# Where a decoder's modulation products stand between its memory attention and its feed-forward

## The chip, the cores and the metric

One core of a Trainium2 chip runs one program. The metric is the device time of one execution in microseconds, as a median of runs. Lower is better.

## The reference, cut to what matters

A first block (sequence of 512 tokens, width 1024) does a mixer, a cross-attention to a memory, and a feed-forward, each added to x. Two layers of a second block follow. Each layer is steered by three vectors (shift, scale, gate) for the tokens and three for a context; they come from a small product of a conditioning vector with `w_mod`, and depend on nothing else.

```python
x = x + memory_cross_attention(rms_norm(x, norm_mem_g), mem, ..., w_mo)   # ends with o @ w_mo
h = rms_norm(x, norm_ffn_g)
x = x + square(relu(h @ w_ff1)) @ w_ff2
...
sc, scc = silu(c), silu(c_ctx)
for i in range(2):
    mod_x = sc @ w_mod[i] + b_mod[i]        # 1024 x 3072
    mod_c = scc @ w_mod[i] + b_mod[i]
    x, ctx = mixer_layer(x, ctx, mod_x, mod_c, ...)
```

## The kernel before, in words

**Weights.** All weights are fp32 in HBM and pass through one stream (class `Stream`, lines 184 to 330). A chunk of 512 KB is loaded into a raw slot by SyncE's queue (L205, `loads`); there are 3 slots at first, 7 from the memory's attention on and 9 after the memory's output projection (`more_raw`). A chunk is split into a high and a low part: one unit of 512 columns (fp32r weights, L266 on ScalarE and L267 on VectorE), or one unit of 1024 columns (feed-forward, fp16, L273 on ScalarE and two L291 on VectorE). The units live in a ring of 9 (`RING`), so a unit can be made only when the one nine before it has been used up by TensorE. A raw slot is free again when its units are split. A product takes three matmuls: high by high, low by high, high by low (L416, L417, L418).

**Scales.** An fp16 unit can be made only when its group of columns has a scale: the sum of squares of each of the group's four chunks is taken on ScalarE (L224, written into the ring tile of the unit just being made, so in two halves of 512 where that unit is fp32r), then `total` adds them up (L428 on VectorE, L430 a small matmul, L431, L432 on GpSimd, L433) and L273 may begin. `pump` takes these sums while it makes units, and looks ahead by four chunks at most:

```python
while n and self.nstat < self.nd and self.nstat <= ci + AHEAD:   # L258, AHEAD = 4
    n -= self.stat(lo)
```

**Order.** The program is a list of steps. A clock kept by hand (`D.clk`) advances by each matmul's estimated cost; at each tick `pump` may make one unit, and chains that are due take their next step (`norm_chain` waits `N1` = 2000 and `ND` = 1300 of it). The frame that builds the program then orders each engine's instructions by its own model of time, so neighbours on an engine can change places.

**The modulation pieces.** `w_mod` of a layer is taken in 6 pieces of 1024 by 512, twelve in all (`mod`, L1439). A piece is four chunks, eight fp32r units (8 of L266, 8 of L267), 16 matmuls of 512 columns (L1444, L1445, L1447), one eviction (L1451, L1452) and one small write on ScalarE's queue (L1453). Nothing reads a layer's six results before all six are there; then `mod_chain` (L1458) works them up and writes `mod_d`. `MODS` names for each of the twelve the place in the program where it stands:

```python
MODS = 'duuhhhhii012'                     # L49
mods = [(n, (1, n) if n < 6 else (0, n - 6)) for n in range(12)]
```

Four stand in the memory's attention (`h`). Two stand between the memory's output projection and the feed-forward (`i`, L2372). One each stands at the ends of the feed-forward's parts 0, 1 and 2.

**Around the change.** The memory's output projection takes two blocks of 512 columns over four token tiles; a token tile of a block is 12 matmuls. With the second block, each tile's sum is added to x (L1238) and its norm begins at once (`norm_x`, `norm_chain`): a square with its sum on ScalarE (L614), six short instructions on GpSimd (L404 to L412), one multiplication on VectorE (L618), eight transposes on TensorE (L630), two copies on ScalarE (L421) and two subtractions on VectorE (L422). Two buffers hold the normed tile, so tile 2 begins when tile 0 has been transposed. Then come the pieces of `i`, then part 0 of the feed-forward's first matrix (`ff1`, L1364), whose first block works on tokens 0 to 255 first (tiles 0 and 1, 48 matmuls of 256 columns), then on tokens 256 to 511. The feed-forward has eight parts of 512 hidden columns, in the order ff1(0), ff1(1), ff2(0), slot 0, ff1(2), ff2(1), slot 1, and so on; after part 4 the context's norm is set up (`ctx_norm0`, L1497), which needs layer 0's six pieces.

Of the kernel before, what the change touches and what calls it, by code (L numbers as in the profile page):

```python
# [45 lines left out]
ZP = 2  # L46
ZPOS = ((0, 0), (0, 1), (0, 2), (4, 0), (4, 2), (4, 3), (5, 3), (5, 4), (6, 2), (7, 3))
VPOS = ((1, 1), (1, 2), (1, 3), (2, 1), (2, 2), (2, 3))
MODS = 'duuhhhhii012'  # L49
RN = 1.2  # L50
RM = 2.24
RA = 0.6
# [279 lines left out]
def decoder_kernel(ctx: ExitStack, tc: tile.TileContext, A: dict, out: bass.AP):  # L332
# [1973 lines left out]
    def add_mod(i, j):  # L2306
        add(lambda b: mod(i, j, b), wblk(A["w_mod_2"][i][:, j * 512:(j + 1) * 512], fr=True))
# [3 lines left out]
    def slot(c):  # L2311
        while mods and MODS[mods[0][0]] == c:
            add_mod(*mods.pop(0)[1])
# [131 lines left out]
```

## Time and profile before

| what | value |
|---|---|
| median of 3 runs | 2428.55 us (2423.89 to 2429.85) |
| the profiled execution | 2421.47 us |
| its span, first to last instruction | 2419.7 us |
| mean granted TensorE clock | 0.978 of full speed |
| VectorE, ScalarE, GpSimd busy | 64%, 54%, 13% of the span |
| DMA | 226.67 MB, 94 GB/s over the span |

The span is the time that the trace covers; the execution's own time has 1.77 us around it. Times in rows are microseconds from the span's start. In the timeline, the length of a matmul includes its run through the array, and the next one starts before it ends: the pace is the distance of starts. A number in square brackets is the time for which the engine sat idle before the row, with the instruction that ended it.

### The profile page before, as it was taken

What the parts mean: (1) busy time and instruction counts of PE and PEld (TensorE: products, weight loads), DVE (VectorE), ACT (ScalarE), POOL (GpSimd) and SP (SyncE); (2) the same over time, 40 slices, a digit from 0 to 9 for tenths busy, and PEclk for the clock granted to TensorE, in tenths of its full rate; (3) what the DMA queues carried; (4) which work ended last, traced back from release to release, by engine and by line L of the source; (5) the groups of instructions that cost most, each with busy time, mean ns of one, the idle gap of its engine ahead of it and who ended that gap; (6) DMA issues with size and microseconds to landing.
All of it is one profiled execution on the core that took longest, in us unless ns stands there. A gap on an engine that the chain in (4) does not pass through costs nothing. (4 is left out here: it accounts for less than half of the span.)

```text
span 2419.7 us, 38066 instructions
## 1 busy us (share of the span) xinstructions
PE 2261.3 (93%) x14342; PEld 1505.2 (62%) x14342; DVE 1544.2 (64%) x3136; ACT 1298.1 (54%) x2745; POOL 320.7 (13%) x703
## 2 busy tenths in 40 slices
PE   7899899899999989999988999999779999899998
PEld 6777687544444557767767566557546567764446
DVE  6878678656665677665777444443777657865543
ACT  5656457746655455535777434323535457775532
POOL 4320321100100211004000000000621121000001
PEclk9899899899999999999999999999989999999999
DMA  4512445534443411112221422211421113233311
GB/s 158 140 47 71 141 144 199 172 101 153 155 140 106 122 50 38 46 40 65 79 74 56 137 79 61 79 42 63 156 86 50 42 38 108 71 115 113 103 44 61
DMA packets 182220, 226.67 MB, mean 94 GB/s; under 512 B 28556, under 2 KB 130876, under 8 KB 182036
## 3 DMA queue, kind: packets, MB, share of 16 engines
q1 hardware_dynamic: 158084, 187.67, 25.1%
q10 hardware_dynamic: 23952, 36.57, 4.4%
q8 instruction: 112, 1.84, 0.3%
q14 instruction: 72, 0.59, 0.1%
HBM read 207.33 MB, written 16.88 MB: 93 GB/s over the span
## 5 line engine op out<-in xcount | busy, mean ns | idle before, releaser
L416 PE MATMUL mm<-hTh,wh 128*128 128x512 f16 (+1 forms) x1040 | 392.6, 378 | 7.3 <-ACT wh L273 3.1
L291 DVE SCALAR_TENSOR_TENSOR wl<-raw,gs,wh 128x512 f16<-128x512 f32 (+2 forms) x420 | 296.6, 751 | 150.6 <-ACT wl L224 116.5
L417 PE MATMUL mm<-hTl,wh 128*128 128x512 f16 (+1 forms) x1040 | 392.4, 377 | 0.0
L418 PE MATMUL mm<-hTh,wl 128*128 128x512 f16 (+1 forms) x1040 | 391.2, 377 | 0.0
L224 ACT ACTIVATE wl<-raw 128x1024 f16<-128x1024 f32 (+3 forms) x242 | 222.9, 921 | 69.6 <-PE mm L417 37.3
L416 PEld LDWEIGHTS <-wh 128*128 128x128 f16 x1712 | 168.0, 98 | 147.4 <-issue 6.8
L417 PEld LDWEIGHTS <-wh 128*128 128x128 f16 x1712 | 168.0, 98 | 146.1 <-issue 9.6
L418 PEld LDWEIGHTS <-wl 128*128 128x128 f16 x1712 | 167.8, 98 | 143.9 <-issue 0.6
L738 ACT ACTIVATE ph<-mm 128x512 f16<-128x512 f32 (+2 forms) x300 | 146.1, 502 | 162.4 <-PE mm L734 156.1
L273 ACT ACTIVATE wh<-raw,gs 128x1024 f16<-128x1024 f32 x156 | 175.3, 1141 | 105.9 <-PE mm L417 83.0
L266 ACT ACTIVATE wh<-raw 128x512 fp32r<-128x512 f32 (+2 forms) x244 | 141.7, 613 | 142.2 <-PE mm L418 49.7
L739 DVE SCALAR_TENSOR_TENSOR pl<-mm,ph 128x512 f16<-128x512 f32 (+2 forms) x300 | 165.9, 567 | 73.6 <-ACT ph L738 71.1
L267 DVE TENSOR_TENSOR wl<-raw,wh 128x512 fp32r<-128x512 f32 (+2 forms) x244 | 156.1, 667 | 55.3 <-ACT wh L266 40.2
L432 POOL TENSOR_TENSOR gs<-gs,nh 128x1 f32<-128x1 f32 x66 | 40.6, 616 | 1125.2 <-DVE gs L431 1079.3
L416 PE MATMUL mm<-wh,hTh 128*128 128x512 f32 (+5 forms) x512 | 181.7, 356 | 5.5 <-DVE vf L1589 2.0
L418 PE MATMUL mm<-wh,hTl 128*128 128x512 f32 (+5 forms) x512 | 180.1, 352 | 1.8 <-DVE hTl L422 1.7
L417 PE MATMUL mm<-wl,hTh 128*128 128x512 f32 (+5 forms) x512 | 180.1, 352 | 0.3 <-DVE wl L267 0.3
L734 PE MATMUL mm<-ident,P 128*128 128x128 f32 x928 | 153.9, 283 | 5.9 <-ACT P L721 2.0
L721 ACT ACTIVATE P<-S,s 128x768 f32<-128x768 f32 (+4 forms) x160 | 105.8, 666 | 35.1 <-PE mm L734 18.0
L734 PEld LDWEIGHTS mm<-ident,P 128*128 128x128 f32 x928 | 108.6, 145 | 19.6 <-ACT P L721 2.9
L2133 DVE SCALAR_TENSOR_TENSOR z<-z,mm 128x256 f32<-128x256 f32 (+1 forms) x72 | 42.8, 596 | 107.2 <-PE mm L418 98.9
L271 POOL TENSOR_SCALAR wh<-raw,gs 128x1024 f16<-128x1024 f32 (+3 forms) x54 | 65.8, 1219 | 328.2 <-PE mm L417 209.9
(503 smaller groups left out, 5360.8 us busy)
## 6 DMA issues: line engine op xcount, KB each, us to landing
raw<-in_w_in_dram SPq DMA_DIRECT2D x124, 512.0 KB, 3.5
raw<-in_w_ff_dram SPq DMA_DIRECT2D x64, 512.0 KB, 4.5
raw<-in_w_mod_dram SPq DMA_DIRECT2D x48, 512.0 KB, 5.1
raw<-in_w_branch_dram SPq DMA_DIRECT2D x24, 512.0 KB, 3.4
raw<-in_w_o_dram SPq DMA_DIRECT2D x16, 512.0 KB, 4.0
raw<-in_cmp_w_dram SPq DMA_DIRECT2D x16, 256.0 KB, 3.5
raw<-in_w_out_dram SPq DMA_DIRECT2D x8, 512.0 KB, 3.6
raw<-in_w_mkv_dram SPq DMA_DIRECT2D x8, 512.0 KB, 3.7
```

Of the source, the lines that this page charges most:

```text
L224: nc.scalar.activation(lo[:, :b - a], t[:, a:b], AF.Square, accum_out=g.t[:, g.cols:g.cols + 1])
L266: nc.scalar.activation(hi[:, :m], src, AF.Copy)
L267: nc.vector.tensor_sub(lo[:, :m], src, hi[:, :m].bitcast(FT))
L273: nc.scalar.activation(hi[:, :m], src, AF.Copy, scale=s)
L291: self.nc.vector.scalar_tensor_tensor(l[:, b], src[:, b], s, h[:, b], op0=OP.mult, op1=OP.subtract)
L416: PE.matmul(ps, ah, bh, start=start, stop=False)
L417: PE.matmul(ps, ah, bl, start=False, stop=False)
L418: PE.matmul(ps, al, bh, start=False, stop=stop)
L721: ACT.activation(P, v[:, j, :], AF.Exp, bias=it.nb[:, j:j + 1], accum_out=it.den[:, j:j + 1])
L734: PE.transpose(ps[:, a - a0, :], it.P[0 if len(it.P) == 1 else j][:, c:c + 128], ident)
L738: ACT.activation(ph[:, :m], ps[:, :m], AF.Copy, scale=PSC)
L739: DVE.scalar_tensor_tensor(pl[:, :m], ps[:, :m], PSC, ph[:, :m], op0=OP.mult, op1=OP.subtract)
```

## The change

Only the string of places differs.

```diff
-MODS = 'duuhhhhii012'
+MODS = 'duuhhhh00123'
```

The pieces keep their order. Layer 0's pieces 1 and 2, which stood at `i`, go to the end of part 0; piece 3 goes from the end of part 0 to that of part 1, piece 4 from part 1 to part 2, and piece 5 from part 2 to part 3. Seen by places, `i` has none instead of two, part 0 ends with two instead of one, parts 1 and 2 end with one as before, and part 3 ends with one instead of none. The stream loads weights in the order of use, so the eight chunks of the two pieces are loaded behind the twelve of ff1(0), ff1(1) and ff2(0) instead of ahead of them, and the sums of squares for ff1(0) are taken while the units of the memory's output projection are made.

## Rows read from the trace of the kernel before

**Rows 1.** The page, part 1: busy us (share of the span) xinstructions.
```profile
PE 2261.3 (93%) x14342; PEld 1505.2 (62%) x14342; DVE 1544.2 (64%) x3136; ACT 1298.1 (54%) x2745; POOL 320.7 (13%) x703
```

**Rows 2.** By stretch: us; PE, PEld, DVE, ACT, POOL busy; clock, DMA share, GB/s.
```profile
443.06:468.87 25.81, 14.96 (x67) 8.46 (x66) 18.52 (x36) 23.31 (x51) 4.30 (x14) 0.77 0.51 164
468.87:482.00 13.13, 13.13 (x97) 10.74 (x97) 11.53 (x21) 12.24 (x19) 0.00 (x0) 0.79 0.69 236
482.00:533.66 51.66, 51.66 (x244) 23.45 (x242) 24.68 (x48) 21.68 (x42) 1.10 (x2) 1.00 0.28 93
533.66:537.55 3.89, 3.89 (x18) 1.53 (x16) 2.55 (x4) 3.72 (x5) 0.00 (x0) 1.00 0.46 135
```

**Rows 3.** Timeline, TensorE: start us, us, line, out<-in xcount [idle before <-releaser].
```profile
444.69 1.03 PE L630 MATMUL S<-ident,xn 128*128 128x128 f32 x8
...
449.43 0.39 PE L1444 MATMUL mm<-wh,ms 128*34 128x512 f32 x1
453.59 1.72 PE L630 MATMUL S<-ident,xn 128*128 128x128 f32 x8 [3.77 <-DVE hTl L422]
...
460.49 0.63 PE L1444 MATMUL mm<-wh,ms 128*34 128x512 f32 x1
...
468.87 0.39 PE L416 MATMUL mm<-hTh,wh 128*128 128x256 f16 x1 [3.06 <-ACT wh L273]
...
474.57 0.27 PE L416 MATMUL mm<-hTh,wh 128*128 128x256 f16 x1
```

**Rows 4.** Timeline: norm of tile 0, of tile 3; splits by source.
```profile
435.86 1.06 ACT L614 ACTIVATE xn<-oc 128x1024 f32<-128x1024 f32 x1 [3.04 <-DVE oc L1238]
...
438.89 0.19 POOL L412 TENSOR_TENSOR s<-s,s 128x1 f32<-128x1 f32 x1
...
439.12 1.28 DVE L618 SCALAR_TENSOR_TENSOR xn<-oc,s,g 128x1024 f32<-128x1024 f32 x1 [0.68 <-POOL s L412]
...
453.06 1.04 ACT L614 ACTIVATE xn<-oc 128x1024 f32<-128x1024 f32 x1
...
L421 ACT ACTIVATE hTh<-S x8: 575/580/597, 447.2 to 463.7; 128x512 f16<-128x512 f32 x8
```

**Rows 5.** Timeline, ScalarE: sums of squares (L224), splits (L266), scaling (L273).
```profile
443.86 0.61 ACT L224 ACTIVATE wl<-raw 128x512 fp32r<-128x512 f32 x1
...
444.47 1.67 ACT L266 ACTIVATE wh<-raw 128x512 fp32r<-128x512 f32 x3
...
458.63 0.62 ACT L224 ACTIVATE wl<-raw 128x512 fp32r<-128x512 f32 x1
...
467.68 8.41 ACT L273 ACTIVATE wh<-raw,gs 128x1024 f16<-128x1024 f32 x8
```

**Rows 6.** Timeline, ScalarE and TensorE around the end of part 0.
```profile
532.75 0.63 ACT L266 ACTIVATE wh<-raw 128x512 fp32r<-128x512 f32 x1 [7.45 <-PE mm L418]
533.83 1.06 ACT L224 ACTIVATE wl<-raw 128x1024 f16<-128x1024 f32 x1 [0.45 <-PE mm L417]
...
546.63 0.17 PE L430 MATMUL S<-sb,onesb 128*128 128x1 bf16 x1
...
547.80 4.27 ACT L273 ACTIVATE wh<-raw,gs 128x1024 f16<-128x1024 f32 x4 [1.00 <-POOL gs L432]
```

**Rows 7.** Timeline, VectorE and TensorE, where the context's norm is put.
```profile
660.78 1.28 DVE L618 SCALAR_TENSOR_TENSOR xn<-ctx,s,g 128x1024 f32<-128x1024 f32 x1 [4.00 <-DMA g<-mod_d]
...
663.12 0.38 PE L416 MATMUL mm<-wh,ffh 128*128 128x512 f16 x1 [2.93 <-DVE oc L1240]
```

**Rows 8.** Weight loads: one issue on SyncE's queue, and issue to landing.
```profile
413.24 9.60 SPq L205 DMA_DIRECT2D raw<-in_w_mod_dram  x7
...
DMA to landing us min/median/max: 3.6/5.2/5.5
```

**Rows 9.** Timeline, TensorE in the memory's attention: a gap, and matmuls after it.
```profile
388.15 0.38 PE L416 MATMUL S<-mkh,mqh 128*128 128x256 f32 x1 [2.01 <-ACT P L721]
...
390.76 0.41 PE L418 MATMUL S<-mkh,mql 128*128 128x256 f32 x1
```

## The prediction

> **What bounds the kernel now.** The first view is the page's busy times: TensorE works through 93% of the span [rows 1], so a change that adds and removes no work can only win or lose where TensorE waits or runs at half clock. The second is the table by stretch. From ff1(0)'s second half to the end of ff2(0) TensorE never stops and has its full clock: 51.66 us for 240 matmuls of 512 columns, 0.215 us each [rows 2]. The stretch ahead of it is the opposite: from the first piece at `i` to the first matmul of ff1(0), 25.81 us hold 14.96 us of TensorE, and the clock is 0.77; the next 13.13 us are busy, but at 0.79 [rows 2]. That is the place that the change empties.
>
> The third view, TensorE's timeline there, shows what the loss consists of. The first piece runs through at full clock until 449.43; then come a gap of 3.77 us, transposes that take 1.72 instead of 1.03 us, modulation matmuls of 0.63 instead of 0.39 us, and a last gap of 3.06 us that ends with a scaling (L273) on ScalarE. Full clock is back by 474.57 [rows 3]. The 1.2 GHz level sets in after the gap and goes after some 5 us of dense work.
>
> What does the work need at full clock? Two pieces at 3.89 us each [rows 2] are 7.8; four groups of transposes at 1.03 [rows 3] are 4.1; ff1(0)'s first block, 96 matmuls of 256 columns at half of 0.215, is 10.3. Together 22.2 of the 38.94 us from 443.06 to 482.00 [rows 2]. **The loss is 16.7 us**: 10.85 of gaps (25.81 less 14.96), about 5.9 at half clock.
>
> **Why it waits there.** ScalarE is busy for 23.31 of the 25.81 us [rows 2]. It does three things at once: it splits the units of the pieces, it takes the sums of squares for ff1(0), and it serves the four norms. The sums lie between the splits from 443.86 to 458.63, and the first scaling begins at 467.68 [rows 5]. Tile 3's square, whose tile was complete at about 443.2, starts at 453.06 [rows 4]. So two causes stand in one place: the pair of pieces with the sums behind it, and the norms.
>
> **The change part by part.**
>
> *Removed from `i`.* 32 matmuls, 16 L266, 16 L267, two evictions, two writes on ScalarE's queue, eight loads of 512 KB on SyncE's. As work this is moved, not saved: 7.8 us of TensorE come back later. What can go is the 16.7 us.
>
> *ff1(0)'s sums come earlier.* They are now taken while the eight units of the output projection are made. The loads of ff1(0) go out where the pieces' did, from 413.24 on, and land 5.2 us later, about 418.4 [rows 8]. The first sum may stand ahead of the projection's first split in ScalarE's order, and hold it until then. Lower bound nothing, upper bound 3 us (a landing from a load that still waits for its slot). I take 0.6, near the lower end, since the order is built by a model of time that can put a split first.
>
> The row behind that risk: at 660.78 a VectorE instruction at the head of its queue waited 4.00 us for a load, and TensorE then waited 2.93 us for the addition behind it [rows 7]. The Trainium skill (TensorE: Matmul & The Clock Gate, section on the architectural detail of the array) says that ScalarE and VectorE take their instructions strictly in order; the trace agrees with that row. By that rule a misplaced sum costs the whole wait; were ScalarE free to pass it, the 0.6 would be zero.
>
> *The norms lose their cover.* One norm takes, from the square's start at 435.86 to the end of L618 at 440.40, 4.5 us, then 1.03 of transposes, two copies of 0.58, and a subtraction of half of L618's 1.28: 7.4 us [rows 3, 4]; with the addition to x ahead, 8.0 from a tile's last matmul. ff1(0) begins with tiles 0 and 1. Tile 1 ends two tiles of 12 matmuls (some 5.8 us) before 443.2, so it is ready at 445.4 at best; two groups of transposes fill most of those 2.2 us, and tile 3, ready at 451.2, is in time for the second half at 452.6. Lower bound of the loss: about 0.2 us. Upper bound: ScalarE is as crowded as before, tile 3's square again begins 9.9 us late, and half clock doubles the first half's 5.2 us: 13 us. ScalarE will be crowded: eight scalings of 1.05 us for ff1(0) and ff1(1) [rows 5], eight sums of some 1.1 to 1.2, and the norms' squares and copies all fall between 430 and 455. So I take 7.5: 5 of gap, 2.5 of half clock.
>
> On the clock the rows differ: after a gap of 2.01 us TensorE's matmuls of 256 columns went to 0.41 us [rows 9], after one of 2.93 they were at full length [rows 7]. The same page of the Trainium skill (Part 1, the HAM clock gate) says that idleness throttles the array to half and sustained work frees it; the trace agrees on both levels. By that rule a gap of some us is charged again; by the row at 663 it is not, and the sum would be 2.5 us better.
>
> *The pair at the end of part 0.* The ring sets the order. Before, the piece's eighth unit could be split only at 532.75, 0.9 us before its first matmul, and the ring tile after it came free at 533.83 [rows 6]. With two pieces, units 9 to 16 have to be made from then on, and the four sums for ff1(2) hang on just these units (look-ahead of four chunks). On ScalarE: 8 splits at 0.52 us pace (1.67 for three, less one's 0.63) and 8 half sums at 0.61 [rows 5, 6]: 9.1 us. The last unit is there at 9.2, with its low part at 9.9 us after the pieces' start; TensorE would want it at 7.3. Then the scale: from L430 to the first scaling 1.17 us [rows 6], one scaling 1.05 [rows 5]. ff1(2) starts 10.6 to 12.6 us after the pieces' start instead of 7.8. Loss 2.8 to 4.8, by how early L430 stands; I take 4.0. Lower bound 0 (the sums are spread earlier), upper bound 10 (the gaps bring half clock, as at `i`).
>
> *The other pieces.* Parts 1 and 2 keep one. Part 0 gets one more and part 3 its first; hidden by nothing, they are the 7.8 us counted above as moved. One piece at a part's end costs no gap [rows 2]. Layer 0's piece 5 ends a part later, so `mod_chain` and the context's norm come later; the stall that they cause [rows 7] goes along. Nothing, within 3 us either way, its size before. The loads on SyncE's queue: eight of them wait behind twelve for the feed-forward, in a stretch where DMA is busy for 0.28 [rows 2]; no cost.
>
> **The sum.** 16.7 less 0.6, 7.5 and 4.0 is a gain of 4.6 us. Against the profiled execution's 2421.47 us that is 2416.9; that execution lies 7.1 us under the median of 2428.55, so against the median it is **2424.0 us**.
>
> **The rivals.**
>
> *The norms are covered.* With the pair gone, ScalarE drains, the transposes come in time, and the pair at part 0 loses only the lower value of 2.8. Loss after: 0.2 to 2 for the norms, 2.8 there; gain 12 to 13.7, time about 2415.5. For it: tile 0's norm ran in 4.5 us when ScalarE was free [rows 4]. Against it: the scalings listed above.
>
> *The stall moves with the pair.* At the end of part 0, TensorE waits for units and scale in one gap long enough to lose its clock; as before, the scaling ends that gap and half clock lasts some 5 us more. There 10 us, at the norms 13 instead of 7.5, with 0.6 at the projection: 23.6 against 16.7, slower by 6.9 us, about 2435.5. It decides where the gap passes the 2 us after which half clock was seen [rows 9]. Against it: part 0 has no norms on ScalarE.
>
> *The change does less than it says*: `i` is emptied, but the scale of ff1(0) still ends the wait. Then nothing is won there and the 4.0 is lost: about 2432.5, within 0.3% too. For this, the loads of ff1(0) would have to land late; they go out ahead of eight other loads and no longer behind them, so I count it in the forecast's case.
>
> **How the numbers follow.** A measurement of this kernel can tell about 0.3%, 7.3 us, from no change. My forecast's case (gain of 0 to 7, or a small loss) has 0.56 and alone reaches from 2421.3 to 2432.5. The covered norms have 0.32, the moved stall 0.12. The range takes the first rival whole, 2413 (16.7 less 0.6 and about 1), and the second to 2434; beyond lie most of the second and little of the first. Faster by over 0.3% 0.32, within 0.56, slower 0.12.
>
> **What would show it.** Right: ff1(0)'s first matmul within 3 to 7 us of the projection's last; a scaling row for ff1(0) before the projection ends; gaps of 3 to 5 us in sum around the second piece at part 0's end, released by L266, L267 or L273; the context's stall again, a part later (192 matmuls of 0.215, 41 us). Wrong: a gap inside the output projection released by a load or by L428; half clock for over 5 us at the end of part 0; or TensorE unbroken through both places.

## The result: slower by 0.7%, and the profile after

| what | before | after |
|---|---|---|
| median of 5 runs each | 2423.89 us (2422.72 to 2429.85) | 2441.72 us (2438.65 to 2449.16) |
| ratio, with its 95% interval | | 1.0071 [1.0054, 1.0087] |
| the profiled execution, its span | 2421.47, 2419.7 us | 2443.78, 2442.0 us |
| mean granted TensorE clock | 0.978 | 0.970 |

The forecast was 2424.0 us, a gain of 4.6. The change lost 17. To see where, the stretch from the output projection's first matmul to the end of the feed-forward is cut in three, and 3.89 us [rows 2] taken off for each piece in it, so that kernels with pieces in different places can be compared:

| stretch, less its pieces (us) | before | after | |
|---|---|---|---|
| A: the projection's first matmul to ff2(0)'s first | 85.1 | 87.2 | +2.1 |
| B: from there to ff1(2)'s last (the end of part 0 lies in it) | 41.5 | 54.5 | +13.0 |
| C: from there to the feed-forward's last | 255.1 | 255.2 | +0.1 |

That is 15.3 us. The rest of the 22.3 between the two spans lies ahead of the projection (4.4 us: it began at 420.18 before and at 424.53 after) and behind the feed-forward (2.7 us). In the kernels below, which are nearly the same program up to the projection, it began anywhere between 419.1 and 423.9, and the part behind the feed-forward varies by over 9 us; so neither is put down to the change.

The page of after, part 1 (busy us, share, instructions), answers to [rows 1]: the same matmuls, and TensorE busy with them for 14.4 us longer, at a lower clock.

```profile
PE 2275.7 (93%) x14342; PEld 1514.1 (62%) x14342; DVE 1545.9 (63%) x3136; ACT 1298.4 (53%) x2753; POOL 320.9 (13%) x703
```

The table by stretch of after (columns as in [rows 2]): the projection, from its end to ff1(0), ff1(0) with ff1(1), the pair with the wait behind it, ff1(2).

```profile
424.53:453.36 28.83, 24.54 (x103) 19.03 (x102) 19.08 (x43) 20.58 (x41) 2.88 (x10) 0.94 0.51 158
453.36:462.73 9.37, 2.77 (x19) 2.27 (x17) 6.83 (x12) 8.46 (x14) 4.13 (x12) 0.67 0.57 186
462.73:511.73 49.00, 46.62 (x258) 26.82 (x258) 25.64 (x47) 20.84 (x36) 3.31 (x7) 0.92 0.29 89
532.26:550.82 18.56, 9.84 (x37) 3.44 (x35) 8.66 (x21) 15.72 (x36) 1.10 (x2) 0.76 0.42 142
550.82:574.04 23.22, 23.22 (x97) 10.12 (x98) 16.70 (x27) 15.59 (x26) 0.00 (x0) 0.90 0.64 206
```

The projection takes 28.83 us instead of 23.04 (420.18 to 443.22), and TensorE, with no pieces to do, stands for 6.6 of the 9.37 us behind it. At the end of part 0, 18.56 us hold 9.84 of TensorE at 0.76 of the clock, where one piece had taken 3.89 at full clock [rows 2]; ff1(2) behind it takes 2.3 us longer than its 20.92 before (537.55 to 558.47).

TensorE's timeline of after, the gaps in both places (columns as in [rows 3]):

```profile
427.02 0.51 PE L417 MATMUL mm<-wl,moh 128*128 128x512 f32 x1 [1.79 <-DVE wl L267]
432.56 0.69 PE L416 MATMUL mm<-wh,moh 128*128 128x512 f32 x1 [2.50 <-DVE z L1452]
...
462.73 0.59 PE L416 MATMUL mm<-hTh,wh 128*128 128x256 f16 x2 [4.53 <-ACT hTh L421]
...
541.17 0.40 PE L1445 MATMUL mm<-wl,ms 128*2 128x512 f32 x1 [3.70 <-DVE wl L267]
544.47 0.59 PE L1445 MATMUL mm<-wl,ms 128*2 128x512 f32 x1 [2.05 <-DVE wl L267]
549.49 0.19 PE L430 MATMUL S<-sb,onesb 128*128 128x1 bf16 x1 [1.84 <-DVE sb L428]
550.82 0.61 PE L416 MATMUL mm<-hTh,wh 128*128 128x512 f16 x1 [1.14 <-ACT wh L273]
```

And ScalarE's timeline of after, the same two places, answering to [rows 4 to 6]:

```profile
438.25 1.06 ACT L224 ACTIVATE wl<-raw 128x1024 f16<-128x1024 f32 x1 [4.07 <-DMA raw<-in_w_ff_dram]
...
446.38 1.06 ACT L614 ACTIVATE xn<-oc 128x1024 f32<-128x1024 f32 x1
...
448.49 1.06 ACT L224 ACTIVATE wl<-raw 128x1024 f16<-128x1024 f32 x1 [0.96 <-DMA raw<-in_w_ff_dram]
...
450.75 1.06 ACT L224 ACTIVATE wl<-raw 128x1024 f16<-128x1024 f32 x1 [1.11 <-DMA raw<-in_w_ff_dram]
...
457.46 4.25 ACT L273 ACTIVATE wh<-raw,gs 128x1024 f16<-128x1024 f32 x4
461.62 1.06 ACT L421 ACTIVATE hTh<-S 128x512 f16<-128x512 f32 x2
...
540.91 1.04 ACT L224 ACTIVATE wl<-raw 128x1024 f16<-128x1024 f32 x1
...
541.95 1.04 ACT L224 ACTIVATE wl<-raw 128x1024 f16<-128x1024 f32 x1
...
543.60 0.61 ACT L224 ACTIVATE wl<-raw 128x512 fp32r<-128x512 f32 x1
...
544.70 1.06 ACT L224 ACTIVATE wl<-raw 128x1024 f16<-128x1024 f32 x1 [0.39 <-DMA raw<-in_w_ff_dram]
...
548.10 1.06 ACT L224 ACTIVATE wl<-raw 128x1024 f16<-128x1024 f32 x1 [2.25 <-DMA raw<-in_w_ff_dram]
...
549.63 1.13 ACT L273 ACTIVATE wh<-raw,gs 128x1024 f16<-128x1024 f32 x1
```

At the emptied place the first norm's square (L614) begins at 446.38, and from there to 462 sums (L224) stand between the norms' instructions and wait for their loads (the one at 448.49 is the last of ff1(1)'s, the three behind it are ff2(0)'s); four scalings for ff1(1) (457.46) come ahead of the copy (L421, 461.62) that TensorE waits for. At part 0's end the sums of 1024 columns from 540.91 on belong to ff2(1), the group *behind* ff1(2). Two of them stand ahead of the last half sums of ff1(2) (543.60), all four ahead of ff1(2)'s first scaling (549.63), and two wait for a load. VectorE's low parts (L267) for the last units wait too, because a half sum writes into the ring tile in which the low part belongs:

```profile
543.73 1.31 DVE L267 TENSOR_TENSOR wl<-raw,wh 128x512 fp32r<-128x512 f32 x2 [2.61 <-ACT wl L224]
```

The loads, from SyncE's queue of after (answers to [rows 8]):

```profile
417.62 33.98 SPq L205 DMA_DIRECT2D raw<-in_w_ff_dram  x11
```

Before, the first seven loads of the pieces went out in 9.60 us [rows 8]; here eleven of the feed-forward take 33.98, one in 3.1 us. (The feed-forward's own loads were no faster before: nine went out in the 27.02 us from 433.44 on.) For 29.5 of these us SyncE's queue waited for VectorE's half of a split (15.6 for L267, 13.9 for L291), with which a raw slot comes free. So a sum that looks far ahead waits for a load that had waited for a split: ScalarE waited for five of these loads, 8.0 us in all.

### The profile page after: what moved, and what is told of

Same layout as the page of the kernel before. It is cut to its first block, busy times and chain, and to the rows that moved or that the text cites. A ratio compares the mean times of both kernels' runs of the same rounds, so it can differ in the third digit from the quotient of the medians.

```text
span 2442.0 us, 38059 instructions
## 1 busy us (share of the span) xinstructions
PE 2275.7 (93%) x14342; PEld 1514.1 (62%) x14342; DVE 1545.9 (63%) x3136; ACT 1298.4 (53%) x2753; POOL 320.9 (13%) x703
## 4 chain that ended last, share of the span: by engine, by line
PE 38%; DVE 4%; ACT 4%; issue 2%; POOL 1%; DMA 1%; ACTq 0%; DVEq 0%; POOLq 0%
PE mm L416 11%; PE mm L417 11%; PE mm L418 10%; PE O L755 1%; PE mm L734 1%; DVE wl L291 1%; ACT P L721 1%; ACT wl L224 1%; ACT ph L738 1%; PE S L416 1%; DVE pl L739 1%; PE S L418 0%; PE S L417 0%; ACT wh L273 0%; DVE s L705 0%
## 5 line engine op out<-in xcount | busy, mean ns | idle before, releaser
L291 DVE SCALAR_TENSOR_TENSOR wl<-raw,gs,wh 128x512 f16<-128x512 f32 (+2 forms) x420 | 296.6, 752 | 146.7 <-ACT wl L224 109.3
L224 ACT ACTIVATE wl<-raw 128x1024 f16<-128x1024 f32 (+3 forms) x246 | 223.8, 910 | 73.9 <-PE mm L417 30.5
L273 ACT ACTIVATE wh<-raw,gs 128x1024 f16<-128x1024 f32 x156 | 175.0, 1141 | 102.8 <-PE mm L417 84.9
L266 ACT ACTIVATE wh<-raw 128x512 fp32r<-128x512 f32 (+2 forms) x244 | 141.8, 613 | 155.7 <-PE mm L418 65.3
L267 DVE TENSOR_TENSOR wl<-raw,wh 128x512 fp32r<-128x512 f32 (+2 forms) x244 | 157.0, 669 | 68.3 <-ACT wh L266 50.9
L705 DVE TENSOR_REDUCE s<-S 128x1 f32<-128x768 f32 (+4 forms) x112 | 97.5, 875 | 20.8 <-PE S L418 13.3
```

The costliest lines, as they stand in the source:

```text
L224: nc.scalar.activation(lo[:, :b - a], t[:, a:b], AF.Square, accum_out=g.t[:, g.cols:g.cols + 1])
L266: nc.scalar.activation(hi[:, :m], src, AF.Copy)
L267: nc.vector.tensor_sub(lo[:, :m], src, hi[:, :m].bitcast(FT))
L273: nc.scalar.activation(hi[:, :m], src, AF.Copy, scale=s)
L291: self.nc.vector.scalar_tensor_tensor(l[:, b], src[:, b], s, h[:, b], op0=OP.mult, op1=OP.subtract)
```

## The experiments

Ratios are to the kernel before, on the same chip, with 95% intervals. A, B and C are the stretches of the table above, as differences from before in the profiled execution.

| kernel | A | B | C | ratio |
|---|---|---|---|---|
| the change | +2.1 | +13.0 | +0.1 | 1.0071 [1.0054, 1.0087] |
| e1_spread | +2.0 | 0.0 | -4.2 | 0.9988 [0.9978, 0.9997] |
| e2_pair_only | -1.2 | +12.1 | -1.2 | 1.0042 [1.0027, 1.0057] |
| e3_one_at_i | -5.7 | 0.0 | -1.6 | 0.9963 [0.9949, 0.9977] |
| e4_thin_sums | +2.0 | +7.3 | -1.3 | 1.0032 [1.0021, 1.0044] |
| e5_early_sums | +1.9 | +14.7 | -0.3 | 1.0074 [1.0060, 1.0088] |
| e6_late_next_sums | +0.7 | +9.1 | -0.4 | 1.0046 [1.0032, 1.0059] |
| e7_spread_thin | +2.5 | 0.0 | -3.9 | 0.9995 [0.9986, 1.0005] |
| e8_spread_chain_late | +2.2 | +0.1 | -4.1 | 0.9991 [0.9980, 1.0003] |
| e9_pair_both | +0.9 | -0.2 | -1.9 | 1.0008 [0.9996, 1.0019] |
| e10_spread_hold | -9.2 | 0.0 | -4.1 | 0.9939 [0.9923, 0.9954] |
| e11_one_hold | -7.6 | 0.0 | -1.2 | 0.9966 [0.9955, 0.9977] |
| e12_before_hold | -3.8 | 0.0 | +1.1 | 0.9978 [0.9967, 0.9988] |
| e13_change_both | -7.5 | +0.4 | +1.6 | 0.9958 [0.9944, 0.9971] |

### First: which of the two places

**e1_spread.** Nothing at `i`, no two pieces together.

```diff
-MODS = 'duuhhhh00123'
+MODS = 'duuhhhh01234'
```

> Nothing at the emptied place, as in the changed kernel, but layer 0's five late pieces stand one by one at the ends of parts 0 to 4, so no two are neighbours. Theory P (the loss is the pair at part 0's end, 13.0 us beyond the added piece): that place goes back to what it was (from ff2(0)'s first matmul to ff1(2)'s last, 45 to 46 us), the emptied place still wins nothing (2 us lost), and the time is 2 to 5 us over the kernel before, a ratio of 1.001 to 1.002. Rival E (the emptied place is what costs; the gaps at part 0's end are only its consequence, because the feed-forward starts with a ring and slots that run later): part 0's end still holds some 8 us of gaps with a single piece, and the ratio stays at 1.005 or more.

Part 0's end is what it was before, to the hundredth; the table by stretch:

```profile
447.78:456.89 9.11, 2.04 (x17) 1.63 (x16) 6.82 (x12) 8.16 (x14) 3.82 (x12) 0.88 0.53 188
...
526.74:530.63 3.89, 3.89 (x18) 1.53 (x16) 2.55 (x4) 3.72 (x5) 0.00 (x0) 1.00 0.45 135
```

B is as before, A still lost 2.0: theory P. The ratio fell under the expected one because C won 4.2 us, which no theory had. With piece 5 at the end of part 4, VectorE's L618 of the context's norm (736.58 here, answering to [rows 7]) no longer waits for `mod_d`; in all four kernels with piece 5 there (e1, e7, e8, e10) C is 3.9 to 4.2 us better.

**e2_pair_only.** Both pieces stay at `i`, pieces 3 and 4 form the pair.

```diff
-MODS = 'duuhhhhii012'
+MODS = 'duuhhhhii001'
```

> The two pieces stay where they were before, ahead of the feed-forward, and only the pair is made: pieces 3 and 4 both at the end of part 0, piece 5 at that of part 1. Theory P: the pair alone costs 13 us at part 0's end, less what one piece fewer at part 2 hides (nothing), so the ratio is 1.004 to 1.006, and the gaps at part 0's end are those of the changed kernel (TensorE idle for 8 to 9 us between the first piece and ff1(2)). Rival E: a pair that follows a feed-forward with the old start costs 4 us or less, ratio below 1.002.

B lost 12.1 us, with TensorE's gaps those of the change:

```profile
543.91 0.59 PE L1445 MATMUL mm<-wl,ms 128*2 128x512 f32 x1 [3.70 <-DVE wl L267]
547.21 0.59 PE L1445 MATMUL mm<-wl,ms 128*2 128x512 f32 x1 [1.44 <-DVE wl L267]
...
553.57 0.61 PE L416 MATMUL mm<-hTh,wh 128*128 128x512 f16 x1 [1.17 <-ACT wh L273]
```

So the pair costs 12 to 13 us by itself, whatever stands at `i`.

**e3_one_at_i.** One piece at `i`, four at the ends of parts 0 to 3.

```diff
-MODS = 'duuhhhh00123'
+MODS = 'duuhhhhi0123'
```

> One piece stays ahead of the feed-forward as cover for the norms, the other four late ones stand one by one at the ends of parts 0 to 3. Theory P with the norms uncovered (my step for the norms): one piece covers 3.9 of the 9.4 us between the projection's last matmul and ff1(0)'s first, the sums lie less between its units than between those of two, and no pair is left: 3 to 8 us under the kernel before, ratio 0.997 to 0.999. Rival S (the emptied place is bound by ScalarE's sums and splits together, wherever they are put): the stall in front of ff1(0) keeps its 16 to 17 us with one piece as with two or none, ratio 0.999 to 1.002.

A won 5.7 us and C 1.6; the ratio came out just under the range. One piece in that place is better than two and than none: either the norms need cover, or something stands in their way when it is gone.

### Second: the end of part 0

**e4_thin_sums.** The changed kernel with an eighth of the columns in the sums of ff1(2) and ff2(1). (Its lines stand 4 further on: L270 is L266, L277 is L273, and a sum is L223.)

```diff
+        if getattr(g, "thin", False):
+            nc.scalar.activation(lo[:, :128], t[:, 0:128], AF.Square, scale=float(m / 128) ** 0.5, accum_out=g.t[:, g.cols:g.cols + 1])
+            g.cols += 1
+            m = 0
...
+        g.thin = c in (2,)
...
+        g.thin = c in (1,)
```

> The changed kernel, but the sums of squares for the groups of ff1(2) and ff2(1) are taken over the first 128 of each chunk's 1024 columns (and multiplied by 8), so that each is one short instruction: this leaves out seven eighths of that work. Theory P, with ScalarE's sums as the cause of the stall: eight half sums of 0.61 us and four of 1.06 to 2.1 us turn into eight of about 0.2 us, some 7 us of ScalarE leave the stretch ahead of the last units, and 7 to 11 of the 13.0 us come back, ratio to the kernel before 1.002 to 1.004. Rival U (the units themselves, 16 splits through a ring of 9, set the end; sums or not): at most 3 us come back, ratio 1.006 or more. Rival D (the stall is that of loads that land late): nothing comes back, and ScalarE's wait for a load grows by what the sums gave up.

B came down from +13.0 to +7.3: 5.7 came back, under the 7 to 11 that P forecast, though the ratio lies in its range. The pair itself now ran without a gap that counts (8.2 us). What was left stood behind it, in ScalarE's timeline:

```profile
534.17 0.31 ACT L223 ACTIVATE wl<-raw 128x128 f16<-128x128 f32 x1 [0.52 <-DMA raw<-in_w_ff_dram]
...
536.52 0.31 ACT L223 ACTIVATE wl<-raw 128x128 f16<-128x128 f32 x1 [1.95 <-DMA raw<-in_w_ff_dram]
...
537.81 0.31 ACT L223 ACTIVATE wl<-raw 128x128 f16<-128x128 f32 x1 [0.88 <-DMA raw<-in_w_ff_dram]
```

ScalarE holds still for loads of ff2(1), while ff1(2)'s scaling stands behind. So the length of the sums (P) and their waits (D) both have a part here.

**e5_early_sums.** Look-ahead 8 for both pieces of the pair.

```diff
-        while n and self.nstat < self.nd and self.nstat <= ci + AHEAD:
+        while n and self.nstat < self.nd and self.nstat <= ci + getattr(u.blk, "ahead", AHEAD):
...
+        if i == 0 and j in (1, 2):
+            blk.ahead = 8
```

> The changed kernel, with a look-ahead of 8 chunks instead of 4 while the units of the pair at part 0's end are made, so the sums for ff1(2) go with the first piece's units, ahead of the stop that the ring of 9 makes, in a stretch where ScalarE sat idle for 8 us. Theory P2 (the pair costs so much because the look-ahead of four chunks ties ff1(2)'s sums, and so its scale, to the last eight units): ff1(2)'s first unit is scaled right behind the sixteenth split, the loss at part 0's end falls from 13.0 to between 1 and 4 us, and the ratio is 1.000 to 1.003. Rival U (sixteen splits behind a ring of 9 are the limit, the sums only fill gaps): the loss stays at 8 us or more, ratio 1.004 to 1.007. Rival D (sums that look so far ahead wait for their loads at the head of ScalarE's queue and hold up splits): gaps inside the pieces released by splits, with ScalarE waiting for a load, ratio over 1.003.

A miss, and rival D. ff1(2)'s sums went early as meant, but the second piece's units now took ff2(1)'s sums as well, and ScalarE waited for those loads in the middle of the pair:

```profile
541.14 0.63 ACT L224 ACTIVATE wl<-raw 128x512 fp32r<-128x512 f32 x1 [1.17 <-DMA raw<-in_w_ff_dram]
...
546.84 0.63 ACT L224 ACTIVATE wl<-raw 128x512 fp32r<-128x512 f32 x1 [2.26 <-DMA raw<-in_w_ff_dram]
...
552.58 0.63 ACT L224 ACTIVATE wl<-raw 128x512 fp32r<-128x512 f32 x1 [4.26 <-DMA raw<-in_w_ff_dram]
```

**e6_late_next_sums.** The same new field, for the units of ff1(2) alone.

```diff
+        if c == 2:
+            for b in bl:
+                b.ahead = 0
```

> The changed kernel, but the units of ff1(2) take no sums for the group behind them, so the four sums of ff2(1), which stood ahead of ff1(2)'s first scaling on ScalarE and waited there for loads, come behind it. No work is left out. Theory W (ScalarE's queue: four sums of 1.06 us and 2.6 us of waiting for loads stand between the last split and the first scaling): ff1(2) begins 4 to 6 us sooner after the pieces' start than the 18.6 us of the changed kernel, ratio 1.0045 to 1.006. Rival (the first scaling waits for the scale in any case, whose small matmul stands behind the pieces on TensorE): at most 2 us, ratio 1.006 or more.

ff1(2) began 15.26 us after the pieces' start instead of 18.56. That is 3.3, under the 4 to 6 of theory W; the ratio is in its range. The first gap of 3.7 us, at the low parts, stayed.

**e9_pair_both.** The edit of e6, and that of e5 for the first piece of the pair only.

```diff
+blk.ahead = 8 if (i, j) in ((0, 1),) else AHEAD
...
+[setattr(b, "ahead", 0) for b in bl if c in (2,)]
```

> The changed kernel with two edits at part 0's end and no work left out: the look-ahead is 8 chunks for the units of the first piece of the pair alone (so ff1(2)'s sums go with them, but none of ff2(1)'s with the second piece, whose loads held up ScalarE in the run with 8 for both), and the units of ff1(2) take no sums for the group behind them. Theory P3 (the stall is made of sums: those of ff1(2), tied by the look-ahead of four to the last eight units, and those of ff2(1), standing ahead of the first scaling and waiting for loads): the loss at part 0's end falls from 13.0 to between 1 and 4 us, ratio 1.001 to 1.0035. Rival U (the sixteen splits behind a ring of 9 themselves): the second piece still has gaps before it, released by splits, loss 6 us or more, ratio over 1.004.

By stretch (the pair, then ff1(2)), and in ScalarE's timeline the splits behind the ring's stop with the first scaling:

```profile
528.32:536.37 8.05, 8.05 (x37) 3.21 (x35) 8.05 (x17) 7.64 (x12) 0.00 (x0) 1.00 0.62 186
536.37:556.85 20.48, 20.48 (x97) 9.34 (x97) 13.53 (x26) 17.00 (x29) 0.77 (x1) 1.00 0.64 215
```

```profile
528.71 4.29 ACT L266 ACTIVATE wh<-raw 128x512 fp32r<-128x512 f32 x8 [0.69 <-PE mm L418]
532.90 1.13 ACT L273 ACTIVATE wh<-raw,gs 128x1024 f16<-128x1024 f32 x1
```

B is 0.2 us *under* before, better than the 1 to 4 us of loss that were expected. Two pieces in a row run through at full clock, and the eight splits behind the ring's stop take 4.29 us and hold up nothing: rival U falls. All 13 us at part 0's end were the order of ScalarE's sums, and with them nearly all of the change's loss against before came back (1.0008): at the emptied place the change lost only 2, but it won none of the 16.7 us that stood there.

### Third: the emptied place

**e7_spread_thin.** e1_spread with ff1(0)'s and ff1(1)'s sums over 128 of 1024 columns.

```diff
-        w = lo.shape[-1]
+        m, w, q = (128, 128, (m / 128.0) ** 0.5) if g.thin else (m, lo.shape[-1], 1.0)
...
+        g = Group(); g.thin = c in (0, 1)
```

> The spread kernel (nothing ahead of the feed-forward, one piece at the end of each of parts 0 to 4) with the sums for ff1(0) and ff1(1) over 128 of each chunk's 1024 columns (times 8), which leaves out seven eighths of that work. Theory S (the emptied place wins nothing because the sums, some 9 us of ScalarE, moved under the output projection and the norms): the projection takes 24 to 26 us instead of 28.7, ff1(0) begins sooner behind it, and the time is 5 to 8 us under the spread kernel, ratio to the kernel before 0.995 to 0.997. Rival D (ScalarE stands at the sums waiting for their loads, and VectorE for the vectors of layer 1's chain; the sums' own length matters little): at most 2 us better, ratio 0.998 or more.

A miss. The projection did fall, to 23.91 us, but the wait behind it grew from 9.11 to 14.79: A is no better. Three of ScalarE's waits for loads in that place:

```profile
427.78 0.31 ACT L224 ACTIVATE wl<-raw 128x128 f16<-128x128 f32 x1 [2.58 <-DMA raw<-in_w_ff_dram]
...
432.66 0.31 ACT L224 ACTIVATE wl<-raw 128x128 f16<-128x128 f32 x1 [4.48 <-DMA raw<-in_w_ff_dram]
...
440.96 0.31 ACT L224 ACTIVATE wl<-raw 128x128 f16<-128x128 f32 x1 [2.26 <-DMA raw<-in_w_ff_dram]
```

In this place a shorter sum only waits longer for its load: rival D.

**e8_spread_chain_late.** e1_spread with layer 1's `mod_chain` behind ff2(0).

```diff
+            (i, j) != (1, 0) or DVE.tensor_copy(m[:, 0, 0], X["x"][:, 3, 1016:1024])
...
+        slot(str(c)); c != 0 or add(lambda: spawn(("mod", 1), mod_chain(1)))
```

> The spread kernel, with layer 1's chain (its load, additions and scale) put behind ff2(0) by one small copy, so that VectorE no longer waits 3.5 us for the chain's load in the first half of the output projection. No work is left out. Theory V (that wait, harmless before because the ring stood full, now holds up the low parts of the projection's weights and costs its 2.7 us gap and some 3 us of half clock behind it): the projection falls from 28.7 to 23 to 25 us, ratio to the kernel before 0.9965 to 0.998. Rival (ScalarE sets the pace there with sums and splits; the wait only overlaps): the projection stays over 27 us, ratio 0.998 to 0.9995.

Half a hit. The projection, then the wait behind it:

```profile
423.87:448.39 24.52, 22.79 (x101) 17.78 (x99) 14.91 (x29) 17.75 (x36) 1.74 (x5) 1.00 0.50 160
448.39:462.20 13.81, 3.18 (x19) 2.59 (x18) 9.91 (x16) 11.07 (x18) 5.55 (x15) 0.65 0.53 180
```

The projection fell by 4.2 us, and the wait grew by 4.7. In all eight kernels with nothing at `i` and ScalarE's order there as it was (the change, e1, e4 to e9) ff1(0) starts 37.1 to 38.7 us after the projection's start, whether the projection takes 24 or 29. Something beside TensorE sets that point.

**e10_spread_hold.** e1_spread, with ff1(1)'s sums tied to tile 3's transposed values.

```diff
-            g.t = self.scalep.tile([128, 16], FT, tag="gs", name="gs")
+            g.t = self.scalep.tile([128, 16], FT, tag="gs", name="gs"); self.late(g)
...
+stream.hold, stream.late = held, lambda g: g is held[0].grp and DVE.tensor_copy(g.t[:, 0:8], hB(7, 504, 512)[1])
...
+[setattr(b, "ahead", 0) for b in bl if c in (0,)]
```

`held` are ff1(1)'s blocks, whose units are not made until the last norm is through. So the edit moves more than ff1(1)'s four sums behind the norms: ff1(1)'s four scalings and the sums of ff2(0), which are taken with ff1(1)'s units, go there too.

> The spread kernel with ff1(1)'s sums put behind the last norm (a small copy ties them to tile 3's transposed values), so that ScalarE's squares and copies for the norms stand behind no sum that waits for its load. No work is left out. Theory Q (the emptied place wins nothing because those sums, at the head of ScalarE's queue, wait for loads while the norms' instructions stand behind them): ff1(0)'s first matmul comes 5 to 7 us behind the projection's last instead of 9.1, its second half no longer waits, and the time is 4 to 8 us under the spread kernel's, ratio to the kernel before 0.9955 to 0.9975. Rival N (the chain of the norms, two buffers and 7.4 us each, sets the start in any case): at most 2 us better, ratio 0.998 or more. Rival L (ff1(1)'s units then come late and its block waits for its scale): a new gap of over 2 us ahead of ff1(1), released by a scaling.

Better than expected: 0.9939, A 11.2 us under e1_spread. By stretch (the projection, the wait, ff1(0) with ff1(1)), and TensorE's timeline:

```profile
419.81:444.94 25.13, 23.16 (x103) 17.96 (x102) 19.08 (x42) 14.69 (x30) 4.90 (x14) 1.00 0.64 193
444.94:448.69 3.75, 1.96 (x16) 1.55 (x15) 3.05 (x4) 2.83 (x6) 1.01 (x4) 1.00 0.63 211
448.69:495.76 47.07, 45.52 (x258) 26.10 (x258) 28.86 (x57) 33.20 (x62) 4.23 (x12) 0.96 0.32 108
```

```profile
446.92 1.09 PE L630 MATMUL S<-ident,xn 128*128 128x128 f32 x8 [1.10 <-DVE xn L618]
448.69 0.38 PE L416 MATMUL mm<-hTh,wh 128*128 128x256 f16 x2 [0.69 <-ACT hTh L421]
...
449.91 0.42 PE L417 MATMUL mm<-hTl,wh 128*128 128x256 f16 x1
...
453.20 0.27 PE L416 MATMUL mm<-hTh,wh 128*128 128x256 f16 x1
```

ff1(0) starts 28.9 us after the projection's start, and the scaling that rival L feared holds TensorE for 0.97 us ahead of ff1(1). How much of the 11.2 us is the sums' waits, their length, or the scalings was not tried apart. It is the fastest version of this study, 0.6% under the kernel before and 1.3% under the change by their ratios.

**e11_one_hold** and **e12_before_hold**: the same order with one piece at `i` (`held` and `ahead`, without the copy) and, as a control, with two (the edit of e10 whole).

```diff
-MODS = 'duuhhhh01234'
+MODS = 'duuhhhhi0123'
```

```diff
-MODS = 'duuhhhh01234'
+MODS = 'duuhhhhii012'
```

> The kernel with one piece left ahead of the feed-forward (0.9963 of the kernel before), with ff1(1)'s sums put behind the transposes of ff1(0)'s tokens. Theory Q: ScalarE still waits there for a load at such a sum (1.05 us) and takes four of them (4.3 us) between the norms; with them gone 2 to 5 us come back, ratio 0.9943 to 0.9955. Rival N: what is left there is the chain of the norms; within 1.5 us of that kernel, ratio 0.9957 to 0.997.

> The control: the kernel before with the same edit (ff1(1)'s sums behind the last norm), both pieces ahead of the feed-forward. Theory Q: here the sums that crowd ScalarE are those of ff1(0), between the units of the pair, and the edit takes away only some 4 us of the work behind them: 1 to 4 us under the kernel before, ratio 0.9983 to 0.9996. Rival G (the edit is good wherever it is put, and the emptied place plays no part): as much as in the spread kernel, 4 to 8 us, ratio 0.9965 to 0.9983.

e11 stands within the interval of e3, as rival N said, but it does not settle the matter: without the copy, four sums still stand ahead of tile 3's last copy on ScalarE (465.32), two of them wait 0.50 and 1.67 us for loads, and TensorE waits 1.59 us for that copy. In the control A won 3.8 us; its ratio, 0.9978, is better than theory Q gave it and falls in the range of rival G, but the edit is worth 11.2 us of A where the place is empty and 3.8 where it is full (by the ratios some 12 and 5 us). So it helps in both, and two to three times as much where the pieces are gone.

### Last: is that all?

**e13_change_both.** The change itself, with the edits of e9 and e10.

```diff
 MODS = 'duuhhhh00123'
...
+blk.ahead = 8 if (i, j) in ((0, 1),) else AHEAD
...
+[setattr(b, "ahead", 0) for b in bl if c in (0, 2)]
```

> The changed kernel itself, its pieces where the change put them, with both orders mended: ff1(1)'s sums behind the last norm, the look-ahead of 8 for the first piece of the pair, no sums taken by ff1(2)'s units. No work is left out. If the two orders of ScalarE's sums are the whole of the cause, the two gains add: at the emptied place what the spread kernel won (some 12 us), at part 0's end 13 to 15, together 24 to 29 us of the changed kernel, ratio to the kernel before 0.995 to 0.9975 and some 3 us over the mended spread kernel for the context's stall, which stands a part sooner. If something else in the changed kernel costs as well (the loads of eight chunks behind twelve, the later chain of layer 0), the ratio stays at 0.998 or more.

0.9958, in the range. The wait ahead of ff1(0), and the pair at part 0's end:

```profile
451.08:454.84 3.76, 1.97 (x18) 1.56 (x16) 3.06 (x4) 2.84 (x6) 1.01 (x4) 1.00 0.63 211
...
521.36:529.41 8.05, 8.05 (x37) 3.21 (x35) 8.05 (x17) 7.64 (x12) 0.00 (x0) 1.00 0.58 184
```

The wait and the pair are what they were in e10 and e9; only the projection takes 28.45 us instead of e10's 25.13, with a gap of 2.45 behind VectorE's L1452 that the change has too. With the pieces exactly where the change put them, 27 us (1.0071 less 0.9958 of 2425) came back by the order of ScalarE's queue. That is more than the change lost, because the edit of e10 helps the kernel before as well. Against the control, which has it too, the mended change is some 5 us faster (0.9958 and 0.9978, on different chips, with intervals that just overlap). So nothing of the loss is left for a third cause.

## Why the prediction was wrong, step by step

The sum was 16.7 less 0.6, 7.5 and 4.0, a gain of 4.6 us; measured in the same terms it is 16.7 less 5.8, 13.0 and 13.0, a loss of 15.1 (A and B). All three costs were too small. The step that failed in each is the account of ScalarE's queue: it counted the work in a stretch, but not which instruction stands ahead of which, nor which of them waits for a load.

- **What bounds it.** Right in kind: only waits and half clock moved, and the pieces themselves moved at their 3.89 us (part 3's is there, C +0.1).
- **"ff1(0)'s sums come earlier", 0.6 us, bounds 0 to 3.** Undersized: the projection lost 5.8. A sum stood ahead of the first split, as feared, and waited 0.94 us; the rest are the gaps of 1.79 and 2.50 us and half clock. The longer one is no sum's: VectorE waited 3.30 us for the load of layer 1's chain (430.87), as it had before (3.53 us, at 427.77) without harm. But e7 and e8 took this loss away and won nothing, since the next wait was already there.
- **"The norms lose their cover", 7.5 us, bounds 0.2 to 13.** It came out at the upper bound: A's loss is 16.7 + 2.1 = 18.8, less 5.8 at the projection leaves 13.0. That the bound fits is luck: its 9.9 and 5.2 add up to 15.1, and the 9.9 starts from tile 3's last product, while its addition to x ended only at 446.03, 7.0 us ahead of the square. The step counted what ScalarE has to *do* (scalings, sums, squares). It did not count that sums and scalings for later groups stand ahead of the norms' instructions, nor that ScalarE waits for loads there. With them behind the norms (e10) A falls by 11.2.
- **"The loads ... no cost".** A term put at nothing. It read DMA's busy share of 0.28 [rows 2] as room. The loads were late all the same, because each waits for a raw slot, and ScalarE waited at the head of its queue with other work behind: 2.6 us at part 0's end, for loads of ff2(1) that stand behind the pieces', and 8.0 us from the projection to ff1(0), where the prediction had allowed for a late load at one sum only. [rows 7] had shown such a wait for VectorE.
- **"The pair at the end of part 0", 4.0 us, bounds 0 to 10.** Measured 13.0. The eight splits and eight half sums were counted right in kind; the splits were even done 6.3 us after the pieces' start (the last three end at 538.55). Left out were the four sums of ff2(1), which the look-ahead takes with ff1(2)'s units: 4.2 us of work and 2.6 of waiting, put ahead of the scaling that ff1(2) needs. Also left out: the low parts that wait for a sum to leave their tile. e9 has neither there and loses nothing.
- **The rivals.** "The stall moves with the pair" named the mechanism and both sizes (10 there and 13 at the norms; measured 13 and 13) and had 0.12. It saw one gap that a scaling ends; there were four, ended by L267 twice, L428 and L273. Its 0.6 at the projection was 5.8, so its 2435.5 was still too low. What spoke against it, that part 0 has no norms on ScalarE, was true and beside the point: ScalarE was busy for 15.72 of the 18.56 us there, in part with sums that nothing needed yet. "The norms are covered" counted on a gain of 14 to 16 us at `i` alone (16.7 less 0.6 and 0.2 to 2; the total of 12 to 13.7 then leaves the 0.6 out); with the queue in order, e10 has 9.2 of it.
- **The context's stall** went along, a part later, as said; VectorE's row of after, beside [rows 7]:

```profile
721.36 1.28 DVE L618 SCALAR_TENSOR_TENSOR xn<-ctx,s,g 128x1024 f32<-128x1024 f32 x1 [1.69 <-DMA g<-mod_d]
```

Its size is not fixed: with piece 5 at the end of part 3, C lies between 1.9 us better (e9) and 1.6 worse (e13); with piece 5 at the end of part 4 the wait is gone and C is about 4 better. The place of piece 5 was not tried by itself.

In the Trainium skill (TensorE: Matmul & The Clock Gate, section on the architectural detail of the array) ScalarE takes its instructions strictly in order. The runs agree: 11.2 us of A by moving sums and scalings behind the norms, with no work left out (e10). The Trainium skill (Perfetto Trace Analysis, section Optimizing Scalar/DVE Operations) says that where these engines are not saturated but make others wait, breaking up instructions may bring work to its end sooner. ScalarE is such an engine here, busy for 53%, but no run broke an instruction up. The nearest made the sums shorter by leaving work out: 0.31 us instead of 1.06 in e7 left A where it was, and in e4 gave back 5.7 us of B.

## What to carry to other kernels

Work that is done ahead of need on an in-order engine is harmless only while its input is there and nothing more urgent stands behind it; count for every such instruction where its load stands, not how busy DMA is. When something that filled a place is moved out, ask what the program's look-ahead will put there instead, and when two equal things are put together, what the look-ahead ties to the last of them. If a stall keeps its end point while the work ahead of it shrinks, stop shortening that work and look for what else arrives at that point.

## What was not expected of the hardware

- A sum over 128 columns takes 0.31 us, over 512 0.63 and over 1024 1.06 (rows of e4, e5 and after): a shorter sum saves less than its columns.
- In e10 TensorE went to half clock behind gaps of 1.10, 0.69 and 0.39 us with short work between them: matmuls of 256 columns take 0.42 us from 449.70 on and 0.27 again from 453.09. In the kernel before, it kept full clock behind one gap of 2.93 us [rows 7]. So the prediction's second rival, which looked for a single gap of over 2 us, had no sure sign.
